# Adaptive max pooling on one core: one store for all outputs but the last load's, and a 60 KB pair of loads at the end

## Chip, cores, metric

One core of one Trainium2 chip runs the kernel alone. The metric is device time of one execution in microseconds (us); a run's median over several executions is quoted with its range. The time to beat is 334.98 us.

## The reference

```python
# x: (32, 256, 4096) float32, output_size = 256
for i in range(256):
    result[:, :, i] = np.max(x[:, :, 16 * i : 16 * i + 16], axis=-1)
```

Sixteen neighbouring numbers give one output: 134.22 MB are read, 8.39 MB written, and 2,097,152 windows of 16 are reduced. Spread over 128 partitions that is 16,384 windows per partition; one window is 64 B of input and 4 B of output. Below, "a load of 1,024" means 1,024 windows in each partition: 64 KB runs, 8.39 MB.

## The kernel before

Seventeen loads go into two halves of a ring buffer; each half is 1,024 windows with a gap of 152, and every other use of a half is moved by 152, so that a load may be issued when only the larger of the two reductions of the buffer's earlier content is done. Outputs gather in `kept` and leave at the end. The input is laid out in two groups, each a contiguous block of DRAM in which a partition owns one long run: 9,340 windows (pitch 583.75 KiB) and 7,044 (pitch 440.25 KiB).

```python
CHUNK, GAP, FIRST = 1024, 152, 128
LOADS_A, LOADS_B = 9, 6
LESS = 4
group_a = [FIRST] + [CHUNK] * (LOADS_A - 1) + [CHUNK - LESS]
last = total - sum(group_a) - LOADS_B * CHUNK            # 900
group_b = [CHUNK] * LOADS_B + [last]
...
low = n_loads % 2 * (CHUNK + GAP)
moved = n_loads // 2 % 2
at = low + moved * GAP
nc.sync.dma_start(out=ring[:, at * W : (at + n) * W], in_=xn)
if n != last:
    cut = CHUNK - GAP if moved else GAP
    parts = [(0, cut), (cut, n)]
    for u, v in parts if moved else parts[::-1]:
        pooled(dst[:, u:v], at + u, v - u)               # 872 first, then 152
else:
    ...
    pooled(last_kept, at, n)
...
nc.scalar.dma_start(out=og[:, full : full + last], in_=last_kept)
tc.no_sync_barrier()
for dst, src in stores:                                  # 9,340 and 6,144 outputs
    nc.sync.dma_start(out=dst, in_=src)
```

All loads and the two big stores are issued by the SP engine and share its DMA queue (q1), in order. The last small store is issued by the ACT engine (q10).

## Time and profile before

| | before |
|---|---|
| median of 3 (range) | 334.98 us (334.89 to 335.07) |
| DMA queue of SP, share of 16 engines | 98.8% |
| VectorE busy | 83% |
| last load: issued, first packet, landed | 291.12, 294.79, 312.76 us |
| last reduction | 312.95 to 328.10 us |
| last store: issued, first packet, last packet ends | 328.12, 330.36, 331.83 us |

Times inside an execution count from the start of the profiled span. The lines of the page, of the chain of waits and of the groups stand in the prediction.

### The profile page before, as it was taken

Reading aid. Unit: us, or ns where it says so; the run is one execution under the profiler, and the core shown is the slowest. Engines: PE = TensorE matmul, PEld = TensorE weight load, DVE = VectorE, ACT = ScalarE, POOL = GpSimd, SP = SyncE. Lnnn points to the kernel's source line nnn. Section 1 sums busy time; section 2 is a strip of 40 time slices with the busy share of each in tenths; the row PEclk is TensorE's granted clock in tenths of the full one; section 3 lists DMA queues with packets and bytes.
Section 4 is the critical chain, followed back from the end, with each engine's and each line's share of the span. In section 5 each row is a group of like instructions: output and inputs, shape, how many; then the busy total and the mean of one; then the engine's idle time right before and its main releaser. Section 6 shows DMA issues by size and latency. Waiting matters only on the chain.

```text
span 333.2 us, 113 instructions
## 1 busy us (share of the span) xinstructions
DVE 276.5 (83%) x32; POOL 0.2 (0%) x4
## 2 busy tenths in 40 slices
DVE  2009979797997979799797979979797998979993
POOL 0000000000000000000000000000000000000000
DMA  9898989899898989899898989899898989899987
GB/s 378 378 504 378 504 378 504 378 409 472 378 504 378 504 378 504 378 417 464 376 502 377 504 378 496 386 425 456 378 504 378 504 378 504 378 458 443 393 386 339
DMA packets 2880, 142.61 MB, mean 428 GB/s; under 512 B 320, under 2 KB 320, under 8 KB 448
## 3 DMA queue, kind: packets, MB, share of 16 engines
q1 hardware_dynamic: 2736, 142.15, 98.8%
q10 hardware_dynamic: 144, 0.46, 0.3%
HBM read 134.22 MB, written 8.39 MB: 428 GB/s over the span
## 4 chain that ended last, share of the span: by engine, by line
DMA 57%; DVE 36%; DVEq 5%; issue 0%; SPq 0%
DMA ring<-in_x_dram 57%; DVE kept L56 36%; DVEq L145 5%; SPq L85 0%
## 5 line engine op out<-in xcount | busy, mean ns | idle before, releaser
L56 DVE TENSOR_REDUCE kept<-ring 128x152 f32<-128x2432 f32 (+3 forms) x31 | 261.4, 8473 | 51.6 <-DMA ring<-in_x_dram 51.6
L56 DVE TENSOR_REDUCE ring<-ring 128x900 f32<-128x14400 f32 x1 | 15.1, 15141 | 0.0
L131 POOL MEMSET const-bfloat16-1.0<- 128x1 bf16 x1 | 0.1, 102 | 0.0
L131 POOL MEMSET const-uint8-127<- 128x1 uint8 x1 | 0.1, 101 | 0.0
L131 POOL MEMSET const-float32-0.0<- 128x1 f32 x1 | 0.1, 99 | 0.2 <-issue 0.2
L131 POOL MEMSET const-float32-1.0<- 128x1 f32 x1 | 0.1, 98 | 0.0
## 6 DMA issues: line engine op xcount, KB each, us to landing
ring<-in_x_dram SPq DMA_DIRECT2D x1, 8160.0 KB, 24.0
ring<-in_x_dram SPq DMA_DIRECT2D x1, 7200.0 KB, 21.6
out_dram<-kept SPq DMA_DIRECT2D x1, 4670.0 KB, 32.4
out_dram<-kept SPq DMA_DIRECT2D x1, 3072.0 KB, 18.1
ring<-in_x_dram SPq DMA_DIRECT2D x1, 1024.0 KB, 4.6
out_dram<-ring ACTq DMA_DIRECT2D x1, 450.0 KB, 4.2
ring<-in_x_dram SPq DMA_DIRECT2D x14, 24.0
```

The costliest lines, as they stand in the source:

```text
L56: nc.vector.reduce_max(out=dst, in_=ring[:, at * W : (at + n) * W].rearrange("p (n w) -> p n w", w=W), axis=mybir.AxisListType.X,)
L131: nc = _bacc.Bacc("TRN2", target_bir_lowering=False, num_devices=1)
L145: with _tile.TileContext(nc) as tc:
```

## The change

The intent: one store instead of two, with runs of 60 KB; for that all outputs but those of the last load must lie in one group, so the partition pitch becomes 963.75 KiB and the last load a contiguous block of its own. The one store has to wait until the last but one load is reduced. To let that happen in time, the last but one load is cut to 956 windows and the last grows from 900 to 964.

```diff
@@ -36,13 +36,12 @@
     CHUNK = 1024
     GAP = 152
     FIRST = 128
-    LOADS_A, LOADS_B = 9, 6
+    FULL = 14
 
-    LESS = 4
-    group_a = [FIRST] + [CHUNK] * (LOADS_A - 1) + [CHUNK - LESS]
-    last = total - sum(group_a) - LOADS_B * CHUNK
-    group_b = [CHUNK] * LOADS_B + [last]
-    assert 0 < last and last * (W + 1) <= CHUNK * W
+    NEXT = 956
+    group_a = [FIRST] + [CHUNK] * FULL + [NEXT]
+    last = total - sum(group_a)
+    assert 0 < last <= CHUNK and last <= GAP * W
 
     pool = ctx.enter_context(tc.tile_pool(name="pool", bufs=1))
     ring = pool.tile([P, 2 * (CHUNK + GAP) * W], fp32, tag="ring", name="ring")
@@ -71,16 +70,14 @@
             ow[span].rearrange("(p n) -> p n", p=P),
         )
 
-    stores = []
     n_loads = 0
-    base = 0
-    for g, loads in enumerate((group_a, group_b)):
+    for g, loads in enumerate((group_a, [last])):
         xg, og = group(sum(loads))
         a = 0
         for n in loads:
             xn = xg[:, a * W : (a + n) * W]
-            dst = kept[:, base + a : base + a + n] if n != last else None
-            if n == FIRST:
+            dst = kept[:, a : a + n] if g == 0 else None
+            if g == 0 and a == 0:
 
                 nc.sync.dma_start(
                     out=ring[:, CHUNK * W : (CHUNK + n) * W], in_=xn
@@ -92,26 +89,27 @@
                 moved = n_loads // 2 % 2
                 at = low + moved * GAP
                 nc.sync.dma_start(out=ring[:, at * W : (at + n) * W], in_=xn)
-                if n != last:
+                if n == CHUNK:
                     cut = CHUNK - GAP if moved else GAP
                     parts = [(0, cut), (cut, n)]
                     for u, v in parts if moved else parts[::-1]:
                         pooled(dst[:, u:v], at + u, v - u)
+                elif g == 0:
+                    pooled(dst, at, n)
                 else:
-                    end = (at + CHUNK) * W
-                    last_kept = ring[:, end - n : end]
+
+                    free = low if moved else at + CHUNK
+                    last_kept = ring[:, free * W : free * W + n]
                     pooled(last_kept, at, n)
                 n_loads += 1
             a += n
-        full = a - last if g else a
-        stores.append((og[:, 0:full], kept[:, base : base + full]))
-        base += full
+        if g == 0:
+            first_og = og
     assert taken == total
 
-    nc.scalar.dma_start(out=og[:, full : full + last], in_=last_kept)
+    nc.scalar.dma_start(out=og, in_=last_kept)
     tc.no_sync_barrier()
-    for dst, src in stores:
-        nc.sync.dma_start(out=dst, in_=src)
+    nc.sync.dma_start(out=first_og, in_=kept)
 
 
 # ---- launch: one core; inputs and outputs as the reference has them ----
```

## The prediction

> **What bounds the kernel now.** I read the page first, then the chain of waits, then the groups by form and busy time by stretches, and last the packet and landing records around the end. The page shows one busy engine and one busy DMA queue:
>
> ```profile
> DVE 276.5 (83%) x32; POOL 0.2 (0%) x4
> q1 hardware_dynamic: 2736, 142.15, 98.8%
> q10 hardware_dynamic: 144, 0.46, 0.3%
> ```
>
> VectorE is busy 83% of the span; the packets of the SP engine's queue (q1) fill 98.8% of the 16 DMA engines' time. So at most a few microseconds lie outside DMA work. The end of the chain of waits (start, duration, what) shows which work ends last:
>
> ```profile
> 271.77 23.96 DMA ring<-in_x_dram
> 295.73 0.02 issue
> 295.75 17.06 DVE kept L56 x2
> 312.81 0.09 issue
> 312.90 15.19 DVEq L145
> ```
>
> The chain is load, two reductions, the last reduction of 15 us (put down to the queue's drain), and then the last small store. Before that it alternates load and reduction, which looks as if VectorE mattered in the middle. It does not: the next two lines are busy time in the steady part and in the tail (columns: stretch, its length, DVE busy, POOL busy, clock, DMA share, GB/s).
>
> ```profile
> 24.75:295.75 271.00, 241.85 (x28) 0.00 (x0) 1.00 1.00 433
> 328.10:333.20 5.10, 0.00 (x0) 0.00 (x0) 1.00 0.59 245
> ```
>
> In the steady part DMA share is 1.00 at 433 GB/s: fourteen loads land 19.36 us apart (271.00 / 14) while the reductions of one load take 14.69 + 2.68 = 17.36 us. Only the last 5 us are loose. The durations come from the groups by form:
>
> ```profile
> L56 DVE TENSOR_REDUCE kept<-ring 128x872 f32<-128x13952 f32 x14 | 205.6, 14686 | 44.3 <-DMA ring<-in_x_dram 44.3
> L56 DVE TENSOR_REDUCE kept<-ring 128x152 f32<-128x2432 f32 x15 | 40.1, 2676 | 0.0
> L56 DVE TENSOR_REDUCE ring<-ring 128x900 f32<-128x14400 f32 x1 | 15.1, 15141 | 0.0
> ```
>
> Slope of the first two: (14686 - 2676) / 720 = 16.68 ns per output window, plus about 140 ns.
>
> The packet records, one packet being one partition's run, give the DMA cost as clearly. Median durations: 65,536 B 2418 ns, 37,360 B (first store) 1382 ns, 24,576 B (second store) 912 ns, 3,600 B (last store) 141 ns. Two of these make a line, 8.4 ns per packet plus 0.03677 ns per byte (27.2 GB/s per engine), and the others fall on it within 1 ns. Loads and stores run at the same price. One engine moves 1/16 of 134.22 + 8.39 MB, which is 8.913 MB: 327.7 us, plus 160 packets at 8.4 ns, 1.3 us, in all 329.1 us. From the first data packet (1.74 us) to the end of the last (331.84 us) there are 330.1 us. The engines therefore idle about 1 us in all, and only by less work or a shorter start or end could time be won.
>
> The end in detail, from the landing records: the last load has landed at 312.76 us, its reduction runs 312.95 to 328.10, its store is issued at 328.12, its first packet starts at 330.36 and its last ends at 331.84, it has landed at 332.34 and the span closes at 333.20. SP's second store ends its packets between 328.7 and 330.7, depending on the engine. So two chains end within a few tenths of each other: the DMA queue running out of work, and reduction plus last store.
>
> **What the Trainium skill says.** "DMA: Bandwidth & Descriptors", section "Where 436 GB/s comes from", gives a ceiling of 435 GB/s for 16 ports; the trace's 433 agrees, so no layout can make the loads faster. The same page, "Latency and other measured facts", warns of HBM row pitch at large powers of two: a copy fell from 207 GB/s per direction at 512 KiB to 103 at 4 MiB, and a few KiB of padding restored it. The two pitches of before, 583.75 and 440.25 KiB, show no such loss here. The same page, "Queues, rings and completion order", says that an engine takes turns between its queues packet by packet, so the last store does not have to wait for all of SP's store; in this trace its packets begin just as SP's end, which neither proves nor denies it. "VectorE: DVE Perf Modes", "The perf-mode tier table", has tensor_reduce at one element per cycle whatever the type; 16 elements in 16.68 ns agree, so larger reductions scale linearly.
>
> **The change, part by part.**
>
> 1. Two stores of kept outputs (9,340 and 6,144 per partition) become one of 15,420 (61,680 B runs). Per engine 16 packets become 8: 8 x 8.4 ns = 0.07 us less. A run costs 8.4 + 61,680 x 0.03677 = 2276 ns; eight of them 18.2 us, against 8 x (1382 + 912) = 18.35 before, of which 64 outputs moved to the last store. Total bytes are unchanged.
>
> 2. The store can no longer start on the first group while the tail is being reduced. Before, the first store was queued at 291.50, long ahead, and followed the last load without a gap. Now everything waits for the reduction of the last but one load. That load is 956 windows instead of 1,024: eight packets per engine shorter by 4,352 B each, 8 x 0.160 = 1.28 us, less the 4 windows that another load no longer saves (0.07): it lands at 295.73 - 1.21 = 294.52. Its single reduction takes 14.686 + 84 x 0.01668 = 16.09 us and ends at 310.63; the store is issued at about 310.75. Issue to first packet took 1.0 us for the first load (0.73 to 1.74) and at most 2.24 us for the last store, so the first store packet is ready between 311.8 and 313.0. The last load's packets end between 312.0 and 312.4. Gap: 0 to 0.8 us, my estimate 0.3.
>
> 3. The last load is 964 windows instead of 900. The sum of all loads is the same, so it lands at 312.76 again. VectorE is free since 310.6, so the reduction starts at 312.79, 0.16 us earlier than before. It takes 15.141 + 64 x 0.01668 = 16.21 us and ends at 329.00 instead of 328.10: 0.90 us later, on the path that sets the end.
>
> 4. The last store: 3,856 B runs, 150 ns instead of 141, eight per engine, +0.07 us. Issued at 329.02, ready 1.3 to 2.24 us later, 330.3 to 331.3. SP's store ends at 312.2 + 18.2 + 0.3 = 330.7, about where it ended before. Whichever is later, the eight packets take some 1.3 us: last packet at 331.9 to 332.6, against 331.84.
>
> 5. Pitch: 963.75 KiB for all but the last load, and a contiguous last load. Four pitches are 3,855 KiB, no multiple of a large power of two, though 68 pitches are 64 MiB less 1 KiB, so a few pairs of the 16 engines may meet at the same place. Pairs need 2 x 27 = 54 GB/s, below even the 103 GB/s that the skill's worst pitch left for all 16. I expect packets of 2418 ns again: 0.
>
> Sum: +0.9 from the longer last reduction, of which up to 0.8 was slack before if the last store had been ready early and was held by SP's packets; -0.1 for packets; +0.1 for a possible gap not absorbed. I choose +0.4 us: 334.98 + 0.4 = 335.4 us.
>
> **Rivals.** *The pitch hurts.* If aliasing lowers the load rate by 3%, 310 us of loads become 319 and the time about 344 us. For it: the skill's measurement, and the near-coincidence at 68 rows. Against it: two unlike pitches before gave the same packet time, and only pairs can coincide. *The store waits.* If the SP store's issue comes a microsecond late and its packets also delay the last store, the time is 336 to 336.5. For it: the margin of part 2 is under a microsecond. Against it: such a gap is covered by the last reduction until 331. *Larger runs pay.* If 60 KB writes go better or the skipped store frees 1 us somewhere, the time is 334. Against it: store packets of 24 and 37 KB already lie on the line of the loads, and the dropped ones cost 8.4 ns each. *Nothing:* 335.0, if the last store was fully hidden behind SP's packets and still is.
>
> **Range and chances.** Part 4 alone gives 335.0 to 335.8; a gap or a late landing adds at most 0.4, packet scatter takes 0.2 off. Eight in ten: 334.7 to 336.2. Two per cent is 6.7 us. Faster by that is nearly excluded, as the DMA engines idle only 1 us and the start and end outside them take 3.1: 0.01. Slower by that needs the pitch: 0.04. Within: 0.95.
>
> **What would show it.** Load packets at 433 GB/s and loads landing 19.36 us apart (part 5); a 956 reduction of 16.1 us ending near 310.6 and SP's store issued just after (part 2); DMA busy without a hole over 0.8 us near 312 (part 2); the 964 reduction of 16.2 us ending near 329.0 (part 3); the last store landing near 332.7 instead of 332.34 (part 4). Longer load periods or long store packets would make the prediction wrong.

## More of the kernel before

One more view of before is needed later: the timeline of its end (start, duration, engine, operation; "q" is an engine's sequencer, here issuing DMAs; in brackets the idle time before and what ended it).

```profile
291.12 0.33 SPq L94 DMA_DIRECT2D ring<-in_x_dram  x1
291.50 21.91 SPq L114 DMA_DIRECT2D out_dram<-kept  x2
295.75 17.28 DVE L56 TENSOR_REDUCE kept<-ring 128x872 f32<-128x13952 f32 x2 [2.07 <-DMA ring<-in_x_dram]
312.95 15.14 DVE L56 TENSOR_REDUCE ring<-ring 128x900 f32<-128x14400 f32 x1
328.12 0.37 ACTq L111 DMA_DIRECT2D out_dram<-ring  x1
```

Read the first line against the third: the last load is issued at 291.12 us, while the load in front of it lands only at 295.73. By the packet records the queue reaches the last load at 294.79, so it had stood in line for 3.67 us. I call this the load's lead.

## The result

| | before | changed |
|---|---|---|
| median of 6 (range) | 335.02 us (334.89 to 335.38) | 335.77 us (335.40 to 336.33) |
| ratio, 95% interval | | 1.0022 (1.0009 to 1.0034) |

A ratio here is the mean time of one kernel's runs over that of the other's in the same rounds, so it is not quite the ratio of the medians. The changed kernel is 0.2% slower, and the interval excludes 1. Note the spread: 0.49 us over six runs before, 0.93 after. The profile fell on the fastest of the six runs of the changed kernel (335.40), so it shows less than the typical loss.

The page of the changed kernel, the lines that answer to those of before:

```profile
DVE 276.5 (83%) x31; POOL 0.2 (0%) x4
q1 hardware_dynamic: 2592, 142.11, 98.6%
```

VectorE's work is the same to a tenth of a microsecond; the queue has 144 packets fewer, and still fills its engines. The last two pieces of the chain of waits over 0.1 us:

```profile
291.29 21.76 DMA ring<-in_x_dram
313.15 16.22 DVE ring L55
```

Before, the last 32 us of the chain (from 295.75) were reductions. Now they are the last load itself, from its issue at 291.29 to its landing at 313.05, and then its reduction. The last load has come onto this chain. (The chain follows instructions and whole transfers; what single packets do at the end comes below.) Busy time by stretches, the steady part:

```profile
24.90:276.56 251.66, 224.62 (x26) 0.00 (x0) 1.00 1.00 433
```

The steady part runs at 433 GB/s as before: thirteen loads take 251.66 us, 251.65 in before. The new pitch costs nothing there. The timeline of the end, with the two changed reductions, to lay beside that of before:

```profile
291.29 0.33 SPq L91 DMA_DIRECT2D ring<-in_x_dram  x1
294.66 16.09 DVE L55 TENSOR_REDUCE kept<-ring 128x956 f32<-128x15296 f32 x1 [0.80 <-DMA ring<-in_x_dram]
310.77 0.35 SPq L112 DMA_DIRECT2D out_dram<-kept  x1
313.15 16.22 DVE L55 TENSOR_REDUCE ring<-ring 128x964 f32<-128x15424 f32 x1 [2.40 <-DMA ring<-in_x_dram]
329.40 0.38 ACTq L110 DMA_DIRECT2D out_dram<-ring  x1
```

The store of 60 KB runs is issued at 310.77; its first packet starts at 311.83, while the slowest engine ends its part of the load at 312.69: no engine stands idle for more than 0.16 us between the two. The last reduction starts 0.20 us later than before and is 1.08 us longer, so its store is issued 1.28 us later (329.40 against 328.12). Yet its first packet starts at 330.28, a little earlier than before (330.36), because on the engines that are done with SP's store it now waits for nothing: 0.88 us after the issue. Before, it came 2.24 us after the issue, and by the packet records only when SP's packets ran out on its engine. So before had at least 2.24 - 0.88 = 1.36 us of slack in the chain of the last store.

The changed kernel has less, but not none. The records do not name the engines, but an engine's packets can be strung together, because each starts about 3 ns before the one in front of it ends. The engine that ended its part of the last load last (312.69; before, 312.40) also ended SP's store last, at 330.88 (before, 330.71), and only then took its eight packets of the last store; they ended at 332.30 (before, 331.83). So in this execution the DMA queue of one engine set the end, and the last reduction still had 330.88 - 330.28 = 0.60 us to spare.

One more thing is in the packet records. Loads and stores take 8.4 ns plus 0.03677 ns per byte. In the last load of the changed kernel two of the first packets took 330 and 517 ns more than that; in before none of the first ones did. The queue reached this load at 293.57, when it had been in line for 2.28 us instead of 3.67.

### The profile page after: what moved, and what is told of

Its sections match the earlier page's. It is cut to its first block, busy times and chain, and to the rows that moved or that the text cites. A ratio compares the mean times of both kernels' runs of the same rounds, so it can differ in the third digit from the quotient of the medians.

```text
span 333.6 us, 111 instructions
## 1 busy us (share of the span) xinstructions
DVE 276.5 (83%) x31; POOL 0.2 (0%) x4
## 4 chain that ended last, share of the span: by engine, by line
DMA 62%; DVE 36%; SPq 0%; issue 0%; DVEq 0%
DMA ring<-in_x_dram 62%; DVE kept L55 31%; DVE ring L55 5%; SPq L91 0%; SPq L82 0%; DVEq L55 0%
## 5 line engine op out<-in xcount | busy, mean ns | idle before, releaser
L55 DVE TENSOR_REDUCE kept<-ring 128x872 f32<-128x13952 f32 (+3 forms) x30 | 260.3, 8714 | 50.5 <-DMA ring<-in_x_dram 50.5
L55 DVE TENSOR_REDUCE ring<-ring 128x964 f32<-128x15424 f32 x1 | 16.2, 16219 | 2.4 <-DMA ring<-in_x_dram 2.4
```

Source lines behind the costliest of these rows:

```text
L55: nc.vector.reduce_max(out=dst, in_=ring[:, at * W : (at + n) * W].rearrange("p (n w) -> p n w", w=W), axis=mybir.AxisListType.X,)
```

## The experiments

Every run below gave correct results, five rounds against the kernel before (e7, e10 and e11 have four runs, the others five). "Lead" is from the issue of the last load to its first packet, "landed" the last load's landing, both from the profiled run.

| run | median (range), us | before beside it | ratio (95%) | lead | landed | last reduction ends |
|---|---|---|---|---|---|---|
| before | 334.98 (334.89 to 335.07) | | | 3.67 | 312.76 | 328.10 |
| changed | 335.77 (335.40 to 336.33) | 335.02 | 1.0022 (1.0009 to 1.0034) | 2.28 | 313.05 | 329.37 |
| e1_two_stores | 337.27 (336.36 to 337.42) | 335.10 | 1.0062 (1.0048 to 1.0076) | 2.30 | 314.15 | 330.47 |
| e2_sizes_of_before | 335.01 (334.90 to 335.05) | 335.10 | 0.9999 (0.9986 to 1.0011) | 3.56 | 312.81 | 328.06 |
| e3_60k_loads_alone | 335.85 (335.69 to 336.64) | 335.10 | 1.0032 (1.0020 to 1.0045) | 2.43 | 314.27 | 330.57 |
| e4_one_store_late | 336.48 (336.37 to 336.72) | 335.10 | 1.0044 (1.0032 to 1.0057) | 3.62 | 312.81 | 328.06 |
| e5_before_plus_64 | 335.16 (334.94 to 335.32) | 335.00 | 1.0002 (0.9989 to 1.0015) | 3.85 | 312.58 | 329.16 |
| e6_after_plus_64 | 336.49 (335.81 to 336.65) | 335.00 | 1.0037 (1.0024 to 1.0049) | 2.08 | 313.55 | 331.13 |
| e7_last_1020 | 339.46 (339.07 to 339.56) | 335.00 | 1.0129 (1.0115 to 1.0143) | 1.34 | 316.17 | 333.42 |
| a8_after_again | 335.60 (335.09 to 336.48) | 335.00 | 1.0025 (1.0012 to 1.0039) | 2.27 | 312.87 | 329.19 |
| e9_963_with_lead | 335.04 (334.97 to 335.15) | 335.05 | 1.0002 (0.9990 to 1.0015) | 3.71 | 312.76 | 329.06 |
| e10_before_late_issue | 338.20 (338.14 to 338.45) | 335.05 | 1.0098 (1.0083 to 1.0114) | 1.59 | 315.98 | 331.15 |
| e11_last_1020_late_store | 338.60 (337.80 to 338.99) | 335.05 | 1.0105 (1.0091 to 1.0119) | 1.41 | 314.96 | 332.14 |
| e12_1016_with_lead | 335.29 (335.24 to 335.40) | 335.05 | 1.0010 (0.9997 to 1.0022) | 3.87 | 312.75 | 329.94 |

The theory I started with, the tail theory: the longer last reduction has used up the slack and now sets the end. Rivals: the pitch, and the merging of the stores.

**e1_two_stores.** The changed kernel, its one store cut in two. (The first part is ready, and issued, at 293.8 us: 2.6 us after the issue of the last load and just after its first packet at 293.53, not before the issue as the expectation says.)

```diff
-    nc.sync.dma_start(out=first_og, in_=kept)
+    for u, v in ((0, 14464), (14464, total - last)):
+        nc.sync.dma_start(out=first_og[:, u:v], in_=kept[:, u:v])
```

> The changed kernel with its one store cut in two (14,464 outputs per partition, ready before the last load is issued, then 956). Tail theory: the end is set by the last reduction (16.2 us) and the last small store, which this does not touch, and the one store already began without a gap; so as the changed kernel, 335.4 to 336.0 us. Merge theory (waiting with all outputs, or 60 KB runs, cost the time): back to 335.0 us. Pitch theory: 335.8, the pitch is unchanged.

Measured 337.27 us: no theory had it. The five runs fall into two groups, 336.36 to 336.44 and 337.27 to 337.42; the profile fell on the fastest. The end of its timeline:

```profile
291.23 0.33 SPq L91 DMA_DIRECT2D ring<-in_x_dram  x1
293.83 17.21 SPq L113 DMA_DIRECT2D out_dram<-kept  x2
314.25 16.22 DVE L55 TENSOR_REDUCE ring<-ring 128x964 f32<-128x15424 f32 x1 [3.58 <-DMA ring<-in_x_dram]
```

The last load, of the same size and issued at the same time, landed at 314.15 instead of 313.05. By the packet records its first packets are stretched as in the changed kernel (up to 0.47 us), and so are six of its last packets, by up to 1.20 us. In the changed kernel, whose store comes at 310.77, no last packet is stretched. That merging the stores costs time is refuted.

**e2_sizes_of_before.** The layout of the changed kernel (pitch 967.75 KiB, last load contiguous) with the old sizes and two stores.

```diff
-    NEXT = 956
+    NEXT = 1020
-    nc.sync.dma_start(out=first_og, in_=kept)
+    for u, v in ((0, 9340), (9340, total - last)):
+        nc.sync.dma_start(out=first_og[:, u:v], in_=kept[:, u:v])
```

> Layout of the changed kernel (last load a contiguous block of its own; partition pitch 967.75 KiB), but loads of the old sizes at the end (1,020 and 900) and two stores as before (9,340 and 6,144). Tail theory: 335.0 us, the last reduction is 15.1 us again and its store is ready before SP's packets end. Pitch theory (any pitch near 1 MiB, or the loss of the second group): 335.8 us.

Measured 335.01 us, as before. A layout of this kind costs nothing; this pitch differs from the changed kernel's by 4 KiB, and the steady part shown above covers the exact one.

**e3_60k_loads_alone.** The kernel before with 961 and 963 windows in its last two loads; the ring's layout in that kernel allows no 964.

```diff
+    last = 963
-    group_b = [CHUNK] * LOADS_B + [last]
+    group_b = [CHUNK] * (LOADS_B - 1) + [961, last]
```

> The kernel before with only its last two loads changed to 961 and 963 windows; old pitches, two stores. Tail theory: as the changed kernel, 335.4 to 336.0 us, last reduction 16.2 us ending near 329.1. Pitch theory and merge theory: 335.0 us.

Measured 335.85 us. The sizes of the last two loads alone, in the old layout and with two stores, bring the loss of the change. But the timeline does not say what I had expected of it (a reduction ending near 329.1):

```profile
291.26 0.33 SPq L95 DMA_DIRECT2D ring<-in_x_dram  x1
314.37 16.20 DVE L57 TENSOR_REDUCE ring<-ring 128x963 f32<-128x15408 f32 x1 [3.43 <-DMA ring<-in_x_dram]
```

The last reduction starts 1.42 us later than in before and ends at 330.57, because the load lands at 314.27. The profile fell on one of the slow executions of this kernel (336.59); its five runs fall into two groups, 335.69 to 335.85 and 336.59 to 336.64.

**e4_one_store_late.** The changed kernel with the old sizes but still one store.

```diff
-    NEXT = 956
+    NEXT = 1020
```

> The changed kernel with 1,020 and 900 windows in the last two loads, so that the one store waits for a reduction that ends only near 312.9 us. Tail theory with a full DMA queue: the store's first packets come near 314.0 while the queue runs dry at 312.0 to 312.4, a hole of 1.7 us that nothing fills: 336.4 to 336.9 us. Rival: the hole is hidden behind the last reduction, which ends at 328.1 as before: 335.0 us.

Measured 336.48 us, as the theory has it. Its timeline:

```profile
295.82 17.15 DVE L55 TENSOR_REDUCE kept<-ring 128x1020 f32<-128x16320 f32 x1 [2.00 <-DMA ring<-in_x_dram]
313.00 0.35 SPq L112 DMA_DIRECT2D out_dram<-kept  x1
328.09 0.37 ACTq L110 DMA_DIRECT2D out_dram<-ring  x1
```

The load's packets end by 312.35 and the store's start at 313.85: a hole of at least 1.5 us on every engine, in a queue that has no spare time, and the kernel is 1.4 us slower. So the change was right to shrink the last but one load if it wanted one store. No packet of this last load is stretched; its lead is 3.62 us and nothing stands behind it.

**e5_before_plus_64.** One more reduction of 64 windows ahead of the last one, in the kernel before.

```diff
+                    pooled(last_kept[:, 0:64], at, 64)
                     pooled(last_kept, at, n)
```

> The kernel before with one more reduction of 64 windows (1.2 us, its result is overwritten) ahead of the last one. In the profile of before the last store is issued at 328.12 and its first packet comes at 330.36, in the changed kernel 329.40 and 330.28, so a store needs at most 0.9 us from issue to first packet and before had some 1.3 us of slack. Tail theory: the extra 1.2 us are absorbed, 335.0 to 335.4 us. Rival, no slack (the last reduction set the end in both kernels): 336.2 us.

Measured 335.16 us, ratio 1.0002. The last lines of its timeline (the x2 are the extra and the last reduction):

```profile
312.76 16.40 DVE L56 TENSOR_REDUCE ring<-ring 128x64 f32<-128x1024 f32 x2
329.19 0.37 ACTq L112 DMA_DIRECT2D out_dram<-ring  x1
```

The last store is issued 1.07 us later than in before, its first packet starts at 330.33 against 330.36, and the time does not move beyond the interval. The slack is there.

**e6_after_plus_64.** The same extra reduction in the changed kernel.

```diff
+                    pooled(last_kept[:, 0:64], at, 64)
                     pooled(last_kept, at, n)
```

> The changed kernel with the same extra reduction of 64 windows. Tail theory: its slack is used up, so the 1.2 us show in full, 336.6 to 337.2 us. Rival (pitch or merge made the difference, and the slack is still there): 335.8 us.

Measured 336.49 us, 0.72 to 0.89 above the two measurements of the changed kernel (335.77, 335.60), just below the range expected. In the changed kernel most of such a delay shows; that a part does not fits the 0.60 us to spare found above. In this profile the last store's first packet starts at 332.03, when SP's store has ended on every engine (331.39): here the last reduction did set the end.

**e7_last_1020.** The changed kernel with 900 and 1,020 windows.

```diff
-    NEXT = 956
+    NEXT = 900
```

> The changed kernel with 900 and 1,020 windows in its last two loads (pitch 960.25 KiB): the last reduction becomes 17.15 us, 0.93 longer. Tail theory: 336.3 to 336.9 us. Pitch theory (68 pitches are no longer within 1 KiB of 64 MiB): 335.0 us. Merge theory: 335.8 us.

Measured 339.46 us, three microseconds above the tail theory and the others. A reduction 0.93 us longer cannot do this. The timeline:

```profile
291.37 0.33 SPq L91 DMA_DIRECT2D ring<-in_x_dram  x1
309.02 0.35 SPq L112 DMA_DIRECT2D out_dram<-kept  x1
316.27 17.15 DVE L55 TENSOR_REDUCE ring<-ring 128x1020 f32<-128x16320 f32 x1 [7.28 <-DMA ring<-in_x_dram]
```

VectorE waits 7.28 us for the last load, which lands at 316.17 although the bytes ahead of it are the same as in before. Of its packets 20 of the earliest are up to 0.96 us too long, and 18 of the last up to 1.41. Besides, four engines stood idle before their first packet of this load, for 0.06, 0.53, 1.65 and 1.71 us. Its issue is where it always is, because it hangs on the reduction that frees its buffer (SP waits for VectorE), but the load in front of it is shorter, so the queue comes to it after 1.34 us. The runs so far fall apart by this lead: 1.3 to 2.4 us in e7, e6, e3, e1 and the changed kernel, 3.6 to 3.9 in before, e2, e4 and e5. That is the lead theory. But they fall apart by the length of the last load too (963 windows or more against 900), since shortening the load in front lengthened the last one.

**a8_after_again.** The changed kernel once more, with no edit.

> The changed kernel once more, for a second profile and its time on this chip. Tail theory: 335.4 to 336.0 us; where the last load lands later than in the kernel before, the last store lands later by the same amount.

Measured 335.60 us (335.09 to 336.48). The profile fell on the fastest run, 335.09:

```profile
312.97 16.22 DVE L55 TENSOR_REDUCE ring<-ring 128x964 f32<-128x15424 f32 x1 [2.21 <-DMA ring<-in_x_dram]
329.22 0.37 ACTq L110 DMA_DIRECT2D out_dram<-ring  x1
```

Here the last load landed at 312.87, and the execution took 335.09 us; in the first profile it landed at 313.05, and it took 335.40. In this one execution, with the last load 0.11 us later than in before, the changed kernel is nearly as fast as before.

Four more runs were to tell the lead from the length of the last load and its reduction.

**e9_963_with_lead.** The kernel before with the shortened load moved to the front: the last reduction is as long as in the changed kernel, the lead is as in before.

```diff
-    group_a = [FIRST] + [CHUNK] * (LOADS_A - 1) + [CHUNK - LESS]
+    group_a = [FIRST, 961] + [CHUNK] * (LOADS_A - 2) + [CHUNK - LESS]
```

> The kernel before with the 961-window load as the second load of all instead of the last but one, and 963 windows in the last. The last reduction is 16.2 us as in the changed kernel, but the last load is issued about 4 us before the queue reaches it, as in before, where the changed kernel and run e3_60k_loads_alone leave 2.4 to 2.9. Lead theory (a load issued too shortly before its turn starts with stretched packets and lands late and unevenly; the longer reduction alone fits into the slack): last load lands at 312.7 to 312.9, time 335.0 to 335.3 us, narrow. Rival, the longer reduction itself costs the time: 335.6 to 335.9 us.

Measured 335.04 us, range 0.18 us, ratio 1.0002.

```profile
289.92 0.33 SPq L94 DMA_DIRECT2D ring<-in_x_dram  x1
312.86 16.20 DVE L56 TENSOR_REDUCE ring<-ring 128x963 f32<-128x15408 f32 x1 [1.02 <-DMA ring<-in_x_dram]
329.10 0.37 ACTq L111 DMA_DIRECT2D out_dram<-ring  x1
```

The last load is issued 3.71 us before its first packet (293.63) and lands at 312.76, to the hundredth as in before; none of its first packets is stretched. The last reduction ends at 329.06 and costs nothing. Against e3, which has the same two sizes in another place, this is the whole loss. The tail theory as I had put it falls.

**e10_before_late_issue.** The kernel before, sizes untouched, with an extra reduction of 128 windows that delays the issue of the last load and of the store right behind it.

```diff
                     parts = [(0, cut), (cut, n)]
+                    if n_loads == 13:
+                        pooled(dst[:, 0:128], at, 128)
                     for u, v in parts if moved else parts[::-1]:
```

> The kernel before, sizes untouched, with an extra reduction of 128 windows (2.3 us) just ahead of the reduction that frees the buffer of the last load, so that this load is issued near 293.4 instead of 291.1 us, 1.8 us before its turn. VectorE has 2.1 us to spare there. Lead theory: its first packets are stretched, it lands 0.3 to 2 us later than 312.76; with 1.3 us of slack behind it, 335.3 to 337 us and a wider spread. Rival, the lead does not matter as long as the queue is not dry: 335.0 us.

Measured 338.20 us, 3.15 above the kernel before. The direction was expected, the size not (at most 337), nor that the spread stays small (0.31 us).

```profile
293.19 0.33 SPq L94 DMA_DIRECT2D ring<-in_x_dram  x1
293.56 19.74 SPq L116 DMA_DIRECT2D out_dram<-kept  x2
316.00 15.15 DVE L56 TENSOR_REDUCE ring<-ring 128x900 f32<-128x14400 f32 x1 [3.06 <-DMA ring<-in_x_dram]
```

The load in front ends its packets at 295.10 and those of the last load begin at 294.77 on the engines that are ahead, so the queue as a whole never ran dry. Four of the 16 engines did: they stood idle for 0.24, 1.33, 1.40 and 2.25 us before their first packet of this load, the latest of which came 3.96 us after the issue. The load lands at 315.98, 3.22 us later than in before: 26 of its packets in the first 8 us are stretched by up to 1.00 us, 20 near its end by up to 1.22 us. Sizes, layout and stores are those of before, and VectorE waits 3.06 us for this load: the later issue does this. (The first store, issued right behind the load, comes 2.06 us later too, but still stands in line 19 us before its turn.)

Why the time is above what I had expected can be read from the stores (KB, then us from issue to landing; the first line is of before, the other two of this run):

```profile
out_dram<-kept SPq DMA_DIRECT2D x1, 3072.0 KB, 18.1
out_dram<-kept SPq DMA_DIRECT2D x1, 3072.0 KB, 21.4
out_dram<-ring ACTq DMA_DIRECT2D x1, 450.0 KB, 4.3
```

SP's second store, issued at 312.96 (before, 313.06), landed at 334.37, 3.17 us later than in before and 3.22 us after the last reduction had ended. On the slowest engine its packets ended at 333.95 (before, 330.71), and only then came those of the last store, until 335.06 (before, 331.83). I had counted on 1.3 us of slack behind the load. That slack belongs to the last reduction; the DMA engines have none, and 3.15 of the 3.22 us show in the time.

**e11_last_1020_late_store.** e7 with an extra reduction of 128 windows that delays the issue of the one store by 2.1 us.

```diff
-    NEXT = 956
+    NEXT = 900
                     pooled(dst, at, n)
+                    pooled(dst[:, 0:128], at, 128)
```

> Run e7_last_1020 (900 and 1,020 windows, 339.4 us) with an extra reduction of 128 windows after that of the last but one load, so that the one store is issued near 311.3 instead of 309.0 us. In e7_last_1020 the last packets of the last load, all in flight when the store was queued behind them, took up to 1.4 us too long; where the store came only at 310.8 they did not. If a store queued behind a load stretches the load's last packets: they are back near 2.41 us, the last load lands 0.8 to 1.4 us earlier, time 337.8 to 338.8 us. Rival, the load's size stretches them: 339.4 us.

Measured 338.60 us, 0.86 less than e7.

```profile
291.11 0.33 SPq L91 DMA_DIRECT2D ring<-in_x_dram  x1
311.09 0.35 SPq L113 DMA_DIRECT2D out_dram<-kept  x1
314.99 17.15 DVE L55 TENSOR_REDUCE ring<-ring 128x1020 f32<-128x16320 f32 x1 [3.93 <-DMA ring<-in_x_dram]
```

Of the load's last packets 3 instead of 18 are stretched by more than 0.1 us, and it lands 1.21 us earlier than in e7. Work that delays a store made the kernel faster. That a store standing behind the load stretches its last packets is what this run shows by its packets. How much of the 0.86 us this is worth stays open: both profiles fell on the fastest execution of their kernel, and on the engine that landed last the last packets were still 1.19 us too long (1.27 in e7), while its idle time and stretched first packets, all before the store was issued, came to 1.69 us instead of 2.54.

**e12_1016_with_lead.** The layout of the changed kernel with the short load (904) at the front, 1,016 windows in the last load and two stores.

```diff
-    NEXT = 956
-    group_a = [FIRST] + [CHUNK] * FULL + [NEXT]
+    group_a = [FIRST, 904] + [CHUNK] * FULL
-    nc.sync.dma_start(out=first_og, in_=kept)
+    for u, v in ((0, 9340), (9340, total - last)):
+        nc.sync.dma_start(out=first_og[:, u:v], in_=kept[:, u:v])
```

> The layout of the changed kernel with 904 windows in the second load of all, 1,016 in the last and two stores as in before: the last load is as large as in e7_last_1020 but is issued 4 us before its turn. Lead theory: it lands near 312.8, its reduction of 17.1 us ends near 330.1, its store is ready near 330.9, half a microsecond after SP's packets end: 335.3 to 335.8 us. Rival, the size or the contiguous last block slows the load: 338 to 339.5 us.

Measured 335.29 us, at the lower edge of the lead theory, against 339.46 for e7 with a last load of nearly the same size.

```profile
288.80 0.33 SPq L90 DMA_DIRECT2D ring<-in_x_dram  x1
312.85 17.09 DVE L54 TENSOR_REDUCE ring<-ring 128x1016 f32<-128x16256 f32 x1 [2.14 <-DMA ring<-in_x_dram]
329.97 0.37 ACTq L109 DMA_DIRECT2D out_dram<-ring  x1
```

With 3.87 us of lead the load lands at 312.75. Its reduction, 1.95 us longer than that of before, costs 0.24 us by the medians: the slack covers most of it (its first packet came at 330.84, 0.25 us after SP's store had ended on every engine).

No run beats the kernel before. By the prediction's sum its engines are busy for 329.1 of 330.1 us, so there was about 0.3% to be had.

## Why the prediction was right, and where not

The time lay in the range (335.4 predicted; 335.77 and 335.60 measured). By its steps:

1. One store for two, 0.07 us: too small to be seen in any run, and nothing contradicts it. Store packets of 61,680 B took 2281 ns in the median (predicted 2276).
2. The last but one load was to land at 294.52, its reduction to end at 310.63, the store to be issued at 310.75 and ready between 311.8 and 313.0: measured 294.63, 310.75, 310.77 and 311.83. The longest hole on any engine was 0.16 us, as against an estimate of 0.3 us. e4 shows what the hole would have cost.
3. "The sum of all loads is the same, so it lands at 312.76 again." This is the step that failed. It landed at 313.05 and 312.87 in the two profiles, both of which fell on fast executions, and 1.4 to 3.4 us late in kernels with a like or a shorter lead (e1, e3, e7, e10). I counted bytes in the queue and did not ask when the load joins it. The length of the reduction, 16.21 us predicted and 16.22 measured, was right; that it lay "on the path that sets the end" was not so in the profiled execution, where it had 0.60 us to spare.
4. The last store was to be ready 1.3 to 2.24 us after its issue; it took 0.88. So the slack of before was 1.36 us, more than the 0.8 that I had allowed for. The two errors lean to opposite sides: with the true slack the longer reduction costs nothing (e5, e9), and with the true landing 0.6 to 0.75 us are lost. The last packet ended at 332.30, inside the predicted 331.9 to 332.6, and "whichever is later" was SP's store: 330.88 on the slowest engine, as against 330.7. But the +0.4 was charged to the longer reduction. In the profiled execution the last packet came 0.47 us later than in before: 0.17 because SP's store ended later on that engine, 0.24 because its first packet of the last store was stretched, 0.06 because the packets are larger. So the sum came out near partly by luck. Two readings behind this part were wrong as well. SP's second store in before ended between 330.36 and 330.71 on the 16 engines, not from 328.7 on. And the last store did have to wait for all of SP's store: in no run did it start on an engine before SP's runs had ended there.
5. The pitch: no effect, as predicted (433 GB/s, median packets 2418 ns before and after).

Shown by runs: the sizes of the last two loads carry the loss (e3, e2); the last reduction's length alone does not (e5, e9); a short lead alone makes the last load land late (e10), and a long one restores it at either size (e9, e12). A late landing is not covered by the slack of the last reduction: e10 has the short reduction of before and still loses 3.15 us. Argued from the profiles, not shown: that the wider spread of the changed kernel is the spread of that landing. The two profiles of the changed kernel (312.87 and 335.09 us; 313.05 and 335.40) and that of e3 (314.27 and 336.59) fit, but no profile of the changed kernel fell on one of its slow executions.

Still open: why a transfer that is queued 1.3 to 2.4 us before its turn starts with stretched packets, and on some engines only after they have stood idle (not in e1 and the first profile of the changed kernel; one engine for 0.07 to 0.38 us in a8, e3 and e6; four or more for up to 2.25 us in e7, e10 and e11); where between 2.4 and 3.6 us the effect ends; and why a store standing behind a load stretches that load's last packets by at most 0.56 us where the lead is long (before, e2, e5, e9, e12) and by up to 1.41 where it is short.

## What to carry to other kernels

Where a DMA queue is full from start to end, look not only at whether it runs dry but at how long each transfer has stood in it before its turn: shortening one transfer takes this time from the next one, whose issue may hang on something else. Measure the slack of the final chain (issue of the last store to its first packet, against the same in a run where nothing is in front of it) before you call a longer last step a cost, and look at the engine that ends last: here a late load cost its full delay through the DMA engines, whatever the reduction had to spare (e10). And if transfers of unequal size are needed, put the short one where the next issue has time to spare: here at the front it was free, next to the end it cost 0.75 us.

## What the Trainium skill lacked or had wrong

- "DMA: Bandwidth & Descriptors": no section says how early a transfer must be queued behind another to start at full speed. In these runs a lead of 3.6 us or more left all first packets of the last load at their normal length; 2.1 to 2.4 us stretched one to five of them, by up to 1.25 us; 1.3 to 1.6 us stretched 12 to 26 by up to 1.0 us, left some engines idle for up to 2.25 us before their first packet, and the load landed 2.2 to 3.4 us late.
- The page has nothing either on a store queued behind a load on the same queue: it stretched the load's last packets by up to 0.56 us with a long lead and up to 1.41 us with a short one; with the store issued 2.1 us later, 3 instead of 18 last packets were stretched (e11 against e7).
- Its section "Latency and other measured facts" gives about 0.6 us to the first byte of a DMA issued from SP or ACT. It does not say from when. With the way free, the profiles show 0.88 us from the start of the issuing instruction to the first packet for ACT (changed kernel) and 0.85 us for SP (e4), and 0.50 us from the end of that instruction for both.
- Its section "Queues, rings and completion order" has an engine take turns between its queues packet by packet, a packet there being some 9 to 17 descriptors. It does not say how this maps onto the packets of a profile, each of which is one partition's run here. Taking turns run by run, as the prediction read it, is not what the runs show. In e4 the last store was issued at 328.09 and, by the 0.88 us above, ready at 329.0 (an estimate); all 16 engines still started one more run of SP's store, of 2.3 us, and its first packet came at 332.20. With the last store already running on other engines, an engine still started two more runs of SP's store in e10 and four in e1. In no run did the last store start on an engine before SP's eight runs had ended there. Nor does SP's whole store count as one packet: in e4, on three engines, one run of the last store came between SP's last run and its semaphore write. What the engines go by stays open.
